# Newton steps moved to GpSimd, zero-padded queries, a sixth weight place and an earlier projection in a two-layer encoder

## The chip, the cores and the metric

The kernel runs on one core of a Trainium2 chip. The metric is the device time of one execution in microseconds; the median of the timed runs is compared. TensorE (PE in the profile) multiplies, VectorE (DVE) and ScalarE (ACT) do the elementwise work, GpSimd (POOL) clears tiles, makes small copies and issues some DMAs, and SyncE (SP) issues most DMAs.

## What is computed

Two layers are applied to 512 prompt rows and 32 sample rows of width 1024, in fp32. The sample rows also attend to 256 cached rows. Each layer has four sublayers, and each is wrapped in an RMSNorm before and after:

```python
def layer(h, p, ...):
    h = h + FFN_RES * rmsnorm(swiglu(rmsnorm(h, g_ff1_pre), w_ff1_gu, w_ff1_down), g_ff1_post)
    m, state = token_mix(rmsnorm(h, g_mix_pre), q_pos, past, w_in, ...)
    h = h + rmsnorm(m, g_mix_post)
    h = h + FFN_RES * rmsnorm(swiglu(rmsnorm(h, g_ff2_pre), w_ff2_gu, w_ff2_down), g_ff2_post)
    gate = jax.nn.sigmoid(rmsnorm(h, g_ple_pre) @ w_ple_gate)
    h = h + rmsnorm((p @ w_ple_proj) * gate, g_ple_post)
```

`token_mix` makes one input projection and runs three groups of heads on it: A, stick-breaking attention with 4 heads of width 64; B, latent attention with 8 heads, whose query comes from a projection `cq` of width 256 that is normed and projected again; and C, forgetting attention with 4 heads of width 64. The groups' outputs are normed and projected by `w_out`. The new keys, values and latents are outputs too.

## The kernel before

Activations are kept transposed: the model width lies on the partitions in 8 tiles of 128, and the 544 rows lie in the free dimension. Those columns are worked on in two parts, 0 to 256 and 256 to 544 (`HALVES`), so that one part's norm can run while TensorE multiplies the other.

Each fp32 product is three passes of a rounded type (`gemm`, lines 238 to 240): a weight and an input are each split into a high and a low part, and high by high, high by low and low by high are added in PSUM. `wh`, `wl`, `wx`, `wy` and `pb` are places for split weights and `xa`, `xb` are the input's parts. A weight is loaded into `raw` by SP, its high part is copied by ScalarE (line 109) and its low part subtracted by VectorE (line 113). A string of letters per phase (`MIX_RING` and the like) says which places follow each other; "p" is a `pb` tile. The `pb` tiles serve the attention weights later.

`Normed` and `Finish` do the norms. `Finish.fill` (lines 303, 304) adds a finished sublayer to `h` and `Normed.chunk` (258, 259) splits the next input, block by block. Sums of squares come from line 211. The factor of a norm (one over the root of the mean square) is made by `rstd` in most places: TensorE sums over partitions into a few columns (165, 167), VectorE makes an integer first guess in three operations (171 to 173) and then three Newton rounds of three operations (175 to 177) on a tile of 128x2 or 96x3, and TensorE turns the result into a row and spreads it (179). There are 20 such calls. Another form, `rstd_wide`, uses ScalarE's logarithm (186 to 200). SwiGLU's products with the factor follow in 346, 348 and 349.

In the mixer, `QK` makes queries and keys of A and C: one projection holds two heads of 64, and the result is scaled on eviction (531, 533) into one tile `kf` of the `m` pool, head 0 in rows 0 to 63, head 1 in rows 64 to 127. `attend_pair` then multiplies query and key for two heads and blocks of 128 queries (395), adds a mask by another matmul (402), and goes on to the softmax. For B, the same line reads 128 rows. In A and C the second head's matmul is held in program order.

The mixer's start takes jobs one by one, with the first part of the columns ahead of the second: queries and keys of A, values of A, and the latent's first projection `cq_job(0, ...)`; the latent's second, `cq_job(1, ...)`, comes later. A scheduler orders the instructions of each engine by its own time simulation, and an engine runs its instructions in that order. `rstd` asks for priority (300).

Of the kernel before, what the change touches and what calls it, by code (L numbers as in the profile page):

```python
# [35 lines left out]
def trunk(ctx: ExitStack, tc, a, outs, depth=2):  # L36
# [6 lines left out]
    MIX = (dict(col=16, st=1, kf=2, lq=2, s=2, cs=1, cb=1, kl=1, bq=1, rk=1), dict(m=14), dict(t=5), dict(pb=4), dict(pa=2))  # L43
# [36 lines left out]
    FFN_RING, DOWN_RING, MIX_RING = "xxyyhhhxx", "hhhxxxx", "hhpph"  # L80
# [73 lines left out]

    def rstd(out, acc, n, last=None, rc=None):
# [5 lines left out]
        with tc.high_priority(300):  # L161
# [12 lines left out]
            for _ in range(3):  # L174
                tt(e, rc, rc, op=ALU.mult)
                tt(e, e, v, op=ALU.mult)
                stt(rc, e, 1.5, rc, op0=ALU.add, op1=ALU.mult)
# [202 lines left out]
    def attend_pair(cb, kind, heads, o, chunk, vget, extra=None):  # L380
# [4 lines left out]
        for b in range(2):  # L385
# [4 lines left out]
            for i in (2 * b, 2 * b + 1):  # L390
# [3 lines left out]
                for e, (_, (q, k)) in enumerate(heads):  # L394
                    one = mm(ss[e][:, 0:w], q[:, q0:q0 + 128], k[:, 0:w], start=True, stop=False)  # L395
                    if e and kind != "B":
                        hold(one)
# [81 lines left out]
    def mix(l, h, x, g_next):  # L479
# [37 lines left out]
        class QK:  # L517
            def __init__(s, col0, scale, slot, dst=None):
                s.col0, s.scale, s.slot, s.dst, s.w = col0, scale, slot, dst, None

            def half(s, i, pbank=prj):
                c0, c1 = HALVES[i]
                if s.w is None:
                    s.w = proj(s.col0)
                    s.kf = unit("m")
                n = c1 - c0
                p = pbank()[:, 0:n]
                gemm(p, s.w, x.xh, x.xl, (c0, c1))
                t = s.kf[:, c0:c1]
                if s.scale == 1.0:  # L530
                    tt(t, p, x.r(c0, c1), op=ALU.mult)
                else:
                    stt(t, p, s.scale, x.r(c0, c1), op0=ALU.mult, op1=ALU.mult)
                if c1 == T:
                    copy(sn[:, s.slot, :], s.kf[:, SEQ:T])
                    if s.dst is not None:
                        nc.gpsimd.dma_start(out=s.dst, in_=s.kf)
# [33 lines left out]
        def attend_qk(kind, js, c, chunk, v, extra=None):  # L571
            q, k = js[c]
            heads = []
            for e in range(2):
                r = slice(e * 64, e * 64 + 64)
                heads.append((2 * c + e, tuple(z.kf[r, 0:SEQ] for z in (q, k))))
# [53 lines left out]
        cq_job(0, 0, fbank)  # L630
        rows_rstd(2, 5)
# [4 lines left out]
        cq_job(0, 1, fbank)  # L636
        set_ring("hhh")
# [235 lines left out]
        set_ring("hhhpp")  # L873
# [233 lines left out]
```

## Time and profile before

| what | value |
|---|---|
| timed runs | 2454.08, 2455.56, 2456.77 us (median 2455.56) |
| profiled execution | 2452.86 us, span 2451.1 us |
| TensorE busy, granted clock | 2382.6 us (97%), 0.985 of full speed |
| VectorE, ScalarE, GpSimd busy | 1379.4 (56%), 1025.6 (42%), 48.8 us (2%) |

Busy time is the time in which the engine had an instruction in work. A low share for GpSimd says that there is room on it, not what its instructions cost. TensorE's share is an average, so what it waits for has to be read stage by stage. The timed runs lie within 2.7 us of each other.

### The profile page before, as it was taken

To read this page: it belongs to the slowest core of one execution; us is meant where nothing else is said; L and a number is where in the kernel's file an instruction comes from. 1 tells how busy PE (TensorE), PEld (TensorE's weight loads), DVE (VectorE), ACT (ScalarE), POOL (GpSimd) and SP (SyncE) were. 2 spreads that over 40 slices of the span, in tenths; PEclk is the share of its full clock that TensorE was granted. 3 is DMA by queue.
4 is the path that set the end of the run, shared out by engine and by line. 5 is a ranking of instruction groups with operands and counts; after the bars stand their busy time and mean duration, and the time that the engine had idled before them with its cause. 6 is when DMAs were issued, how large, how long until landed. Compare 5 with 4: busy or idle time off the path is not lost.

```text
span 2451.1 us, 43918 instructions
## 1 busy us (share of the span) xinstructions
PE 2382.6 (97%) x18022; PEld 2253.3 (92%) x18022; DVE 1379.4 (56%) x3052; ACT 1025.6 (42%) x2163; POOL 48.8 (2%) x116
## 2 busy tenths in 40 slices
PE   8999999999998999999999999999999989999997
PEld 8999999886688999999999999998865989999997
DVE  6344446765757344446863444476667663444466
ACT  5322224566754322224533222245677543222243
POOL 0000000110000000000000000001100000000000
PEclk9999999999998999999999999999999999999998
DMA  5322322222023322322213223122211233323221
GB/s 160 111 81 86 105 70 72 93 88 59 23 80 107 104 88 83 101 85 87 84 47 96 95 80 102 54 94 86 89 51 44 81 94 105 95 75 104 81 70 37
DMA packets 72376, 204.99 MB, mean 84 GB/s; under 512 B 9248, under 2 KB 18088, under 8 KB 72176
## 3 DMA queue, kind: packets, MB, share of 16 engines
q1 hardware_dynamic: 69072, 193.57, 25.4%
q0 software_dynamic: 3104, 8.62, 1.1%
q8 instruction: 141, 2.31, 0.4%
q14 instruction: 59, 0.48, 0.1%
HBM read 188.21 MB, written 11.85 MB: 82 GB/s over the span
## 4 chain that ended last, share of the span: by engine, by line
PE 92%; DVE 4%; DMA 2%; ACT 1%; issue 0%; SPq 0%; DVEq 0%; ACTq 0%
PE acc L238 12%; PE acc L239 12%; PE acc L240 12%; PE prj L238 10%; PE prj L239 10%; PE prj L240 10%; PE pv L238 4%; PE pv L239 4%; PE pv L240 4%; PE acc L395 3%; PE pv L414 2%; PE tr L135 2%; DMA raw<-in_w_ff_gu_dram 1%; DVE z L303 1%; PE prj L556 1%; PE prj L557 1%
## 5 line engine op out<-in xcount | busy, mean ns | idle before, releaser
L109 ACT ACTIVATE wh<-raw 128x1024 fp32r<-128x1024 f32 (+3 forms) x157 | 151.1, 965 | 247.5 <-PE acc L239 108.1
L109 ACT ACTIVATE wx<-raw 128x1024 fp32r<-128x1024 f32 (+3 forms) x149 | 139.5, 936 | 266.4 <-PE acc L239 100.2
L113 DVE TENSOR_TENSOR wl<-raw,wh 128x1024 fp32r<-128x1024 f32 (+3 forms) x157 | 173.6, 1107 | 80.0 <-ACT wh L109 79.3
L113 DVE TENSOR_TENSOR wx<-raw,wx 128x1024 fp32r<-128x1024 f32 (+3 forms) x149 | 159.4, 1070 | 75.1 <-ACT wx L109 74.9
L238 PE MATMUL prj<-xa,wh 128*128 128x256 f32 (+3 forms) x632 | 187.8, 297 | 4.6 <-DVE q L346 2.7
L239 PE MATMUL prj<-xb,wh 128*128 128x256 f32 (+3 forms) x632 | 187.1, 296 | 4.1 <-DVE xb L259 4.1
L109 ACT ACTIVATE m<-q 128x256 fp32r<-128x256 f32 (+1 forms) x192 | 81.9, 431 | 255.0 <-DVE q L349 252.7
L240 PE MATMUL prj<-xa,wl 128*128 128x256 f32 (+3 forms) x632 | 184.3, 292 | 0.0
L238 PE MATMUL acc<-xa,wx 128*128 128x256 f32 (+1 forms) x600 | 174.4, 291 | 5.7 <-ACT wx L109 5.7
L239 PE MATMUL acc<-xb,wx 128*128 128x256 f32 (+1 forms) x600 | 173.8, 290 | 0.0
L240 PE MATMUL acc<-xa,wx 128*128 128x256 f32 (+1 forms) x600 | 173.4, 289 | 0.0
L239 PE MATMUL acc<-xb,wh 128*128 128x288 f32 (+1 forms) x576 | 167.4, 291 | 0.0
L240 PE MATMUL acc<-xa,wl 128*128 128x288 f32 (+1 forms) x576 | 166.8, 290 | 0.0
L238 PE MATMUL acc<-xa,wh 128*128 128x288 f32 (+1 forms) x576 | 166.6, 292 | 0.0
L240 PE MATMUL prj<-xa,wx 128*128 128x288 f32 (+1 forms) x480 | 139.5, 291 | 1.3 <-DVE wx L113 1.3
L238 PE MATMUL prj<-xa,wx 128*128 128x288 f32 (+1 forms) x480 | 140.6, 293 | 0.0
L239 PE MATMUL prj<-xb,wx 128*128 128x288 f32 (+1 forms) x480 | 140.3, 292 | 0.0
L347 ACT ACTIVATE q<-q 128x256 f32<-128x256 f32 (+1 forms) x176 | 74.1, 425 | 143.3 <-DVE q L346 140.8
L239 PEld LDWEIGHTS prj<-xb,wh 128*128 128x128 f32 (+1 forms) x632 | 120.1, 190 | 7.7 <-DVE xb L259 5.9
L238 PEld LDWEIGHTS prj<-xa,wh 128*128 128x128 f32 (+1 forms) x632 | 120.1, 190 | 7.7 <-DVE q L346 3.2
L240 PE MATMUL acc<-xa,wy 128*128 128x288 f32 (+1 forms) x424 | 122.7, 289 | 0.7 <-DVE wy L113 0.7
L238 PE MATMUL acc<-xa,wy 128*128 128x288 f32 (+1 forms) x424 | 123.3, 291 | 0.0
(500 smaller groups left out, 7802.5 us busy)
## 6 DMA issues: line engine op xcount, KB each, us to landing
raw<-in_w_ff_gu_dram SPq DMA_DIRECT2D x174, 512.0 KB, 3.5
raw<-in_w_ff_down_dram SPq DMA_DIRECT2D x64, 384.0 KB, 3.1
raw<-in_w_ff_down_dram SPq DMA_DIRECT2D x64, 320.0 KB, 2.9
raw<-in_w_in_dram SPq DMA_DIRECT2D x22, 512.0 KB, 3.5
raw<-in_w_out_dram SPq DMA_DIRECT2D x16, 512.0 KB, 3.4
raw<-in_w_ple_gate_dram SPq DMA_DIRECT2D x16, 512.0 KB, 3.4
raw<-in_w_v_dram SPq DMA_DIRECT2D x8, 512.0 KB, 3.4
t<-dh SPq DMA_DIRECT2D x16, 144.0 KB, 3.0
```

What stands on the lines that cost most here:

```text
L109: act(out, in_, AF.Copy)
L113: tt(lo, src, f(hi), op=ALU.subtract)
L135: nc.tensor.transpose(out, in_, ident[0:n, 0:n])
L238: mm(p, wh[k], xh[k][:, c0:c1], start=i == 0, stop=False)
L239: mm(p, wh[k], xl[k][:, c0:c1], start=False, stop=False)
L240: mm(p, wl[k], xh[k][:, c0:c1], start=False, stop=i == len(ks) - 1)
L303: stt(t, s.y[c][:, c0:c1], s.g[c], s.R[c0], op0=ALU.mult, op1=ALU.mult)
L347: act(g, g, AF.Silu)
L395: one = mm(ss[e][:, 0:w], q[:, q0:q0 + 128], k[:, 0:w], start=True, stop=False)
L414: one = mm(O[64 * e:64 * e + 64, qs], vget(hd, j), pts[e][:, j, qs], start=j == 0, stop=j == end, skip_group_check=True)
L556: mm(p, x.xh[k][:, c0:c0 + n], s.wh[k], start=k == 0, stop=False)
L557: mm(p, x.xl[k][:, c0:c0 + n], s.wh[k], start=False, stop=False)
```

## The change

Four things are changed. In `rstd`, each Newton round's three VectorE operations become four on GpSimd: the last, which added a constant and multiplied by a tensor, is made of two. The first guess stays on VectorE. A query of group A or C gets two tiles of full height instead of one shared by two heads: each holds one head in its own rows and zeros, set by GpSimd, in the others. The key tile stays shared, so that zeros meet the other head's key. The eviction of such a query is two operations of 64 rows. The hold on the second head's matmul goes. The `m` pool has 11 tiles instead of 14, `kf` one instead of two. The mixer's weight string gets a sixth place, "p", and `pb` six tiles instead of four. `cq_job(1, ...)` moves into the mixer's start.

```diff
--- before.py
+++ after.py
@@ -40,7 +40,7 @@
     COMMON = dict(xa=8, xb=8, y=8, h=8, raw=2, wh=3, wl=3, q=6, z=3, sq=2, r=5, n=6, rc=2)
     COMMON_PS = dict(tr=2, acc=3, prj=2, pv=1)
     FFN = (dict(wx=8), dict(m=12, ph=4), dict(wy=4))
-    MIX = (dict(col=16, st=1, kf=2, lq=2, s=2, cs=1, cb=1, kl=1, bq=1, rk=1), dict(m=14), dict(t=5), dict(pb=4), dict(pa=2))
+    MIX = (dict(col=16, st=1, kf=1, lq=2, s=2, cs=1, cb=1, kl=1, bq=1, rk=1), dict(m=11), dict(t=5), dict(pb=6), dict(pa=2))
     where, count, alias = {}, [0], {}
 
     def open_pools(st, sb_tags, ps_tags, tag):
@@ -77,7 +77,7 @@
             s.st.close()
 
     ring, wn, bn = [], [0], [0]
-    FFN_RING, DOWN_RING, MIX_RING = "xxyyhhhxx", "hhhxxxx", "hhpph"
+    FFN_RING, DOWN_RING, MIX_RING = "xxyyhhhxx", "hhhxxxx", "hhpphp"
     RING_TAGS = dict(x=("wx", "wx"), y=("wy", "wy"), h=("wh", "wl"), p=("pb", "pb"))
 
     def set_ring(names):
@@ -151,6 +151,8 @@
             off += n
         bfs.append(at.pop("b_f")[0])
         gains.append(at)
+
+    ptt, pts = nc.gpsimd.tensor_tensor, nc.gpsimd.tensor_scalar
 
     def rstd(out, acc, n, last=None, rc=None):
 
@@ -172,9 +174,10 @@
             ts(rc.bitcast(I32), v.bitcast(I32), 1, MASK, op0=ALU.arith_shift_right, op1=ALU.bitwise_and)
             ts(rc.bitcast(I32), rc.bitcast(I32), -1, MAGIC, op0=ALU.mult, op1=ALU.add)
             for _ in range(3):
-                tt(e, rc, rc, op=ALU.mult)
-                tt(e, e, v, op=ALU.mult)
-                stt(rc, e, 1.5, rc, op0=ALU.add, op1=ALU.mult)
+                ptt(e, rc, rc, op=ALU.mult)
+                ptt(e, e, v, op=ALU.mult)
+                pts(e, e, 1.5, None, op0=ALU.add)
+                ptt(rc, rc, e, op=ALU.mult)
             for i in range(k):
                 mm(t[:, i * m:i * m + m], rc[:, i:i + 1].to_broadcast([m, 128]), ident[0:m, 0:m], start=True, stop=True)
             if out is None:
@@ -392,9 +395,7 @@
                 w = max(nk, 256) if extra else nk
                 ss = [bank("acc") for _ in heads]
                 for e, (_, (q, k)) in enumerate(heads):
-                    one = mm(ss[e][:, 0:w], q[:, q0:q0 + 128], k[:, 0:w], start=True, stop=False)
-                    if e and kind != "B":
-                        hold(one)
+                    mm(ss[e][:, 0:w], q[:, q0:q0 + 128], k[:, 0:w], start=True, stop=False)
                 for e, s in enumerate(ss):
                     if extra:
                         lq, rk = lqs[e]
@@ -517,24 +518,29 @@
         class QK:
             def __init__(s, col0, scale, slot, dst=None):
                 s.col0, s.scale, s.slot, s.dst, s.w = col0, scale, slot, dst, None
+                s.rows = [slice(0, 64), slice(64, 128)] if dst is None else [slice(0, 128)]
 
             def half(s, i, pbank=prj):
                 c0, c1 = HALVES[i]
                 if s.w is None:
                     s.w = proj(s.col0)
-                    s.kf = unit("m")
+                    s.kf = [unit("m") for _ in s.rows]
+                    if len(s.rows) == 2:
+                        for e in range(2):
+                            nc.gpsimd.memset(s.kf[e][s.rows[1 - e], 0:SEQ], 0.0)
                 n = c1 - c0
                 p = pbank()[:, 0:n]
                 gemm(p, s.w, x.xh, x.xl, (c0, c1))
-                t = s.kf[:, c0:c1]
-                if s.scale == 1.0:
-                    tt(t, p, x.r(c0, c1), op=ALU.mult)
-                else:
-                    stt(t, p, s.scale, x.r(c0, c1), op0=ALU.mult, op1=ALU.mult)
-                if c1 == T:
-                    copy(sn[:, s.slot, :], s.kf[:, SEQ:T])
-                    if s.dst is not None:
-                        nc.gpsimd.dma_start(out=s.dst, in_=s.kf)
+                R = x.r(c0, c1)
+                for t, r in zip(s.kf, s.rows):
+                    if s.scale == 1.0:
+                        tt(t[r, c0:c1], p[r, :], R[r, :], op=ALU.mult)
+                    else:
+                        stt(t[r, c0:c1], p[r, :], s.scale, R[r, :], op0=ALU.mult, op1=ALU.mult)
+                    if c1 == T:
+                        copy(sn[r, s.slot, :], t[r, SEQ:T])
+                if c1 == T and s.dst is not None:
+                    nc.gpsimd.dma_start(out=s.dst, in_=s.kf[0])
 
         def qk_jobs(qcol, kcol, scale, slot, dst):
             return [(QK(qcol + 128 * c, scale, slot + c),
@@ -572,8 +578,7 @@
             q, k = js[c]
             heads = []
             for e in range(2):
-                r = slice(e * 64, e * 64 + 64)
-                heads.append((2 * c + e, tuple(z.kf[r, 0:SEQ] for z in (q, k))))
+                heads.append((2 * c + e, (q.kf[e][:, 0:SEQ], k.kf[0][:, 0:SEQ])))
             attend_pair(cb, kind, heads, o, chunk, v.get, extra)
 
         def cache_kv(kname, vname):
@@ -628,12 +633,14 @@
         for t in range(2):
             va.tile(t, fbank)
         cq_job(0, 0, fbank)
+        cq_job(1, 0, fbank)
         rows_rstd(2, 5)
         ja[0][0].half(1, fbank)
         ja[0][1].half(1, fbank)
         for t in range(2, 5):
             va.tile(t, fbank)
         cq_job(0, 1, fbank)
+        cq_job(1, 1, fbank)
         set_ring("hhh")
         cs, cb, kl = mix_constants()
         attend_qk("A", ja, 0, 0, va)
@@ -870,7 +877,7 @@
         gb = group_norm((2, 3, 4, 5), 512, "h")
         on = {**ga, **gc, **gb}
 
-        set_ring("hhhpp")
+        set_ring("hhhppp")
         acc = unit("r")
         y = [None] * KD
         order = [0, 1, 6, 7, 2, 3, 4, 5]
```

Line numbers move by 2 or 3 and more after the change: the first guess is at 173 to 175, the Newton steps at 177 to 180, the broadcast at 182, the fill at 306, 307, 262, 214, SwiGLU's products at 349, 351, 352, and the head matmuls at 398.

Here is the order on VectorE at the start of the second FFN in the first layer, before the change, from the first Newton step on. `rc` and `n` are the small tiles of the call, `wl` the low part of a weight, `z`, `y` and `xb` the tiles of the fill.

```order
L175 TENSOR_TENSOR n_8632<-rc_8379 128x2
L113 TENSOR_TENSOR wl_8735<-raw_8732,wh_8734 128x1024
L303 SCALAR_TENSOR_TENSOR z_8468<-y_7840,gt_77,r_7833 128x288
L303 SCALAR_TENSOR_TENSOR z_8476<-y_7874,gt_77,r_7833 128x288
L176 TENSOR_TENSOR n_8632<-n_8632,n_8631 128x2
L304 TENSOR_TENSOR y_7840<-t_8470,z_8468 128x288
L304 TENSOR_TENSOR y_7874<-t_8478,z_8476 128x288
L177 SCALAR_TENSOR_TENSOR rc_8379<-n_8632,rc_8379 128x2
L113 TENSOR_TENSOR wl_8801<-raw_8798,wh_8800 128x1024
```

The Newton steps stand one by one among weight splits and the fill. After the change, the same place from the first guess's last operation (175) on:

```order
L175 TENSOR_SCALAR rc_8409<-rc_8409 128x2
L203 SCALAR_TENSOR_TENSOR r_7863<-z_8494,z_8491 128x288
L113 TENSOR_TENSOR wl_8768<-raw_8765,wh_8767 128x1024
L306 SCALAR_TENSOR_TENSOR z_8498<-y_7870,gt_77,r_7863 128x288
L306 SCALAR_TENSOR_TENSOR z_8506<-y_7904,gt_77,r_7863 128x288
L307 TENSOR_TENSOR y_7870<-t_8500,z_8498 128x288
L307 TENSOR_TENSOR y_7904<-t_8508,z_8506 128x288
L113 TENSOR_TENSOR wl_8834<-raw_8831,wh_8833 128x1024
```

The nine steps are gone from VectorE, and the rest follows in the same sequence. The result is made by GpSimd, where the first round of this call stands behind two DMA issues:

```order
L791 DMA h_6870<-in_cache_b_ckv_dram 128x256
L736 DMA q_6495<-in_cache_c_logf_dram 4x256
L177 TENSOR_TENSOR n_8662<-rc_8409 128x2
L178 TENSOR_TENSOR n_8662<-n_8662,n_8661 128x2
L179 TENSOR_SCALAR n_8662<-n_8662 128x2
L180 TENSOR_TENSOR rc_8409<-rc_8409,n_8662 128x2
```

Two more such rounds follow it, with nothing between the twelve steps, and each waits for the one before it.

The second place is the first SwiGLU products that need the factor (`q` from 346 and 348), on VectorE too. Before, they stand here, after most of the fill's second part:

```order
L303 SCALAR_TENSOR_TENSOR z_8516<-y_8103,gt_77,r_7833 128x288
L259 SCALAR_TENSOR_TENSOR xb_8373<-y_8067,gt_77,xa_8365 128x288
L304 TENSOR_TENSOR y_8103<-t_8518,z_8516 128x288
L211 TENSOR_TENSOR r_8377<-r_8377,z_8513 128x288
L303 SCALAR_TENSOR_TENSOR z_8526<-y_8139,gt_77,r_7833 128x288
L346 TENSOR_TENSOR q_8624<-prj_8574,r_8378 128x256
L348 TENSOR_TENSOR q_8625<-pv_8575,r_8378 128x256
L346 TENSOR_TENSOR q_8718<-acc_8668,r_8378 128x256
L348 TENSOR_TENSOR q_8719<-prj_8669,r_8378 128x256
```

After the change, the same products (349, 351) stand here:

```order
L262 SCALAR_TENSOR_TENSOR xb_8400<-y_7904,gt_77,xa_8392 128x288
L214 TENSOR_TENSOR r_8407<-r_8407,z_8513 128x288
L307 TENSOR_TENSOR y_7996<-t_8518,z_8516 128x288
L113 TENSOR_TENSOR wx_8840<-raw_8837,wx_8839 128x1024
L349 TENSOR_TENSOR q_8654<-acc_8604,r_8408 128x256
L351 TENSOR_TENSOR q_8655<-prj_8605,r_8408 128x256
L349 TENSOR_TENSOR q_8751<-acc_8701,r_8408 128x256
L306 SCALAR_TENSOR_TENSOR z_8526<-y_8061,gt_77,r_7863 128x288
L351 TENSOR_TENSOR q_8752<-acc_8702,r_8408 128x256
```

They have moved ahead of the fill, from behind tile 6 of 8 of the fill (`y_8103`) to behind tile 3 of 8 (`y_7996`) and a weight split.

The third place is TensorE at the mixer's start in the first layer, where the first part of the columns ends and the second (128x288) begins. `prj_4969` is A's first query projection, `acc_4924` the latent's first. Before:

```order
L238 MATMUL acc_4924<-xa_4570,wh_4917 128x256
L239 MATMUL acc_4924<-xb_4578,wh_4917 128x256
L240 MATMUL acc_4924<-xa_4570,wl_4918 128x256
L238 MATMUL prj_4969<-xa_4563,wh_4760 128x288
L239 MATMUL prj_4969<-xb_4571,wh_4760 128x288
L240 MATMUL prj_4969<-xa_4563,wl_4761 128x288
```

After the change, `acc_4934` is the latent's first projection, `prj_4972` its second, with its weights in `pb`, and `prj_5087` the values of the next rows:

```order
L242 MATMUL acc_4934<-xb_4584,wh_4927 128x256
L243 MATMUL acc_4934<-xa_4576,wl_4928 128x256
L241 MATMUL prj_4972<-xa_4576,pb_4966 128x256
L242 MATMUL prj_4972<-xb_4584,pb_4966 128x256
L243 MATMUL prj_4972<-xa_4576,pb_4967 128x256
L562 MATMUL prj_5087<-pb_4859,xa_4569 128x256
L563 MATMUL prj_5087<-pb_4859,xb_4577 128x256
```

The latent's second projection now runs in the first part, beside the first, and the value projection of the second part starts ahead of A's query.

## Rows read from the trace of the kernel before

**Rows 1.** The page: busy time by engine, and the chain that ended last, by engine.

```profile
PE 2382.6 (97%) x18022; PEld 2253.3 (92%) x18022; DVE 1379.4 (56%) x3052; ACT 1025.6 (42%) x2163; POOL 48.8 (2%) x116
...
PE 92%; DVE 4%; DMA 2%; ACT 1%; issue 0%; SPq 0%; DVEq 0%; ACTq 0%
```

**Rows 2.** Waits of TensorE: line waited for: us in total, times, longest us.

```profile
PE tr L179 <- DVE rc L177: 18.2, 3, 8.3
...
PE prj L239 <- DVE xb L259: 4.1, 7, 1.0
PE tr L179 <- DVE n L177: 3.0, 2, 2.4
PE prj L238 <- DVE q L346: 2.7, 2, 1.3
...
PE prj L238 <- ACT xa L258: 1.9, 2, 1.1
```

**Rows 3.** Timeline of TensorE, first mixer: start us, us, engine, line, operation, shapes.

```profile
471.02 0.30 PE L238 MATMUL prj<-xa,wh 128*128 128x288 f32 x1
471.25 1.12 PE L395 MATMUL acc<-m,m 64*128 64x512 f32 x2
472.31 0.23 PE L402 MATMUL acc<-cb 128*128 128x128 bf16 x1
...
514.42 0.49 PE L395 MATMUL acc<-m,m 64*128 64x128 f32 x4
...
608.33 0.28 PE L240 MATMUL prj<-m,wl 128*128 128x256 f32 x1
608.45 1.02 PE L395 MATMUL acc<-xb,m 128*128 128x512 f32 x2
609.31 0.22 PE L402 MATMUL acc<-cb 128*128 128x128 bf16 x1
```

**Rows 4.** Line 395, head matmuls: duration ns min/median/max, first and last start, forms.

```profile
L395 PE MATMUL acc<-m,m x128: 272/481/694, 456.4 to 1805.2; 64*128 64x256 f32 x48, 64*128 64x384 f32 x32, 64*128 64x512 f32 x32, 64*128 64x128 f32 x16
```

**Rows 5.** Busy us of PE, PEld, DVE, ACT, POOL; granted clock, DMA share, GB/s.

```profile
490.00:540.00 50.00, 50.00 (x361) 42.70 (x360) 35.15 (x72) 30.38 (x71) 11.14 (x28) 1.00 0.29 93
750.00:760.00 10.00, 1.22 (x4) 0.93 (x4) 9.53 (x25) 5.35 (x11) 0.00 (x0) 0.62 0.55 171
760.00:770.00 10.00, 9.59 (x62) 9.59 (x63) 8.75 (x24) 5.54 (x13) 0.00 (x0) 0.70 0.01 2
```

**Rows 6.** Timeline of VectorE, second FFN's start, first layer.

```profile
743.54 0.15 DVE L171 TENSOR_SCALAR n<-tr 128x2 f32<-128x2 f32 x1
...
744.96 0.15 DVE L175 TENSOR_TENSOR n<-rc 128x2 f32<-128x2 f32 x1
...
759.94 0.42 DVE L346 TENSOR_TENSOR q<-prj,r 128x256 f32<-128x256 f32 x1
```

**Rows 7.** Groups on GpSimd: busy us, mean ns of one, idle before.

```profile
L645 POOL MEMSET rk<- 128x512 f32 x2 | 1.1, 553 | 0.0
```

**Rows 8.** Timeline of TensorE, second FFN's start, both layers; idle time in brackets.

```profile
757.86 1.22 PE L179 MATMUL tr<-cst,rc 128*128 128x128 f32 x4 [8.30 <-DVE rc L177]
760.41 0.58 PE L238 MATMUL prj<-xa,wh 128*128 128x256 f32 x1 [1.33 <-DVE q L346]
...
1974.78 1.23 PE L179 MATMUL tr<-cst,rc 128*128 128x128 f32 x4 [6.89 <-DVE rc L177]
```

**Rows 9.** Line 669, copies on GpSimd: duration ns min/median/max.

```profile
L669 POOL COPY s<-kl x32: 202/204/507, 489.5 to 1712.6; 32x32 f32<-32x32 f32 x32
```

**Rows 10.** Line 669 in three stretches: length, GpSimd busy (records), clock, DMA, GB/s.

```profile
490.00:491.45 1.45, 1.29 (x3) 1.00 0.82 308
491.45:492.20 0.75, 0.61 (x3) 1.00 0.09 27
```

**Rows 11.** Timeline at the end, VectorE and TensorE.

```profile
2438.25 0.16 DVE L175 TENSOR_TENSOR n<-n 96x3 f32<-96x3 f32 x1
...
2440.00 1.59 PE L179 MATMUL tr<-cst,n 96*128 96x96 f32 x6 [2.38 <-DVE n L177]
```

## The prediction

> **What bounds the kernel now.** I read the page first, for who is busy and which chain ended last. TensorE is busy 97% of the span and makes up 92% of the chain; GpSimd is busy for 48.8 us of 2451 [rows 1]. So time can come from two places only: matmuls that take longer than their columns need, and the 68 us or so (2451.1 less 2382.6) in which TensorE does nothing. Next I read what TensorE waited for, longest first [rows 2]: the broadcast of the Newton result is at the top, 18.2 us in 3 waits and 3.0 in 2 more, then the second half of the normed input at the mixer's start (4.1 us on xb, 1.9 on xa), and two waits of 2.7 in all for the first SwiGLU tiles. A few waits hold much of it, so I opened each in the timeline. Last I compared head matmuls of the 64-wide groups, which read 64 rows, with those of the latent group, which read 128 [rows 3]. A change in 64 matmuls can't be seen in shares; it must be counted.
>
> The sum is made against the profiled execution, 2452.86 us (span 2451.1 and 1.76 around it). The median of the timed runs is 2455.56, 2.7 higher; what is saved is taken off that. Anything within 0.2%, 4.9 us, counts as no change.
>
> **Zero rows under the 64-wide queries.** The lone 64-row matmul of 512 columns starts 0.23 after its predecessor's start (471.02 to 471.25) and the next matmul starts 1.06 later. The full-height one starts 0.12 after its predecessor and is followed after 0.86 (608.45 to 609.31) [rows 3]. Each predecessor alone is worth 0.13 and 0.12 (288 and 256 columns at the steps in the same rows' neighbours), so the difference is 0.10 + 0.20 = 0.30 us, although a full-height one multiplies twice the rows. The record count says 128, two passes each, so 64 matmuls [rows 4]; one row of adjacent heads is shown, four records in 0.43 us at 514.42 [rows 3], and I found four such pairs in the order. The other 56 stand alone: 56 x 0.295 = 16.5 us. The adjacent ones win nothing: four full-height passes of 128 columns at 0.11 would take 0.44. TensorE has no idle time here (50.00 of 50 us [rows 5]), so a shorter matmul moves the rest forward; but heads also wait for softmax pieces, and some of those waits will appear. I take 14.5; bounds 0 (the extra time belongs to something else than the row count) and 16.5.
> What it adds: 16 more evictions on VectorE of some 0.42 us (the row at 759.94 of 256 columns [rows 6]), 6.7 us in stretches where VectorE is busy 35 of 50 us [rows 5]; hidden by the 15 idle ones. Without that cover they would cost 6.7. Sixteen memsets at about 0.55 [rows 7] run on GpSimd, which is idle; the eight small ScalarE copies likewise go into idle time.
>
> **Newton steps on GpSimd.** VectorE runs nine steps per call, one at a time between other work. At the second FFN's start of the first layer they begin at 744.96, the sums having been read at 743.54 [rows 6], and the broadcast is released only at 757.86 after 8.30 us of idle TensorE; a further 1.33 follows until the first SwiGLU product. In the second layer the same stall is 6.89 [rows 8]. Between those two times VectorE does 9 x 0.16 = 1.4 us of Newton and 11.5 of something else: in the order shown, 21 other instructions are queued between the steps. On GpSimd nothing else is queued.
> The price p of one dependent GpSimd step isn't in the trace. From below: the 32x32 copies, 204 ns in the median [rows 9], start at every 0.25 us in a stretch in which VectorE is idle (three in 0.75). From above: three copies filled 1.29 of a 1.45 us stretch in which VectorE ran two-input operations, 0.43 each [rows 10], the longest 507 ns. VectorE itself was not slower there. I take p = 0.40, nearer the upper row, since VectorE is crowded wherever the result is urgent. Twelve steps: 4.8 us.
> At the two FFN starts: the seed is ready at about 744.7, plus 0.3 to hand over and 4.8, so 749.8 instead of 757.8: 8.0 earlier. In the changed order the SwiGLU products also stand directly behind a weight split, before the rest of the fill, so the 1.33 doesn't grow. The slow clock behind the stall (granted 0.62 and 0.70 of full speed in the two stretches after 750 [rows 5]) cost 2 to 3 us more. Against that, the fill of the second half ends no sooner, at about 766, so TensorE meets that next. I take 8.5 and, from 6.89, 6.5: 15 for both layers. Bounds 8 (p = 0.60 and the fill late) and 22 (8.30 + 1.33 + 6.89 + 1.33 and some 4 of clock).
> The other calls: of 20, three more waited before, 3.05, 0.62 and 2.38 us (the rest of the two sums in [rows 2]). From the changed order I counted the matmuls between a call's last sum and its broadcast, at 0.118 and 0.130 each: 17 calls (without the two above and the last) have 4.6 to 7.7 us, 109.5 in all. A call needs 2.2 + 12p: 0.5 for the sums, 0.6 to 1.4 for three VectorE steps (743.54 to 744.96 [rows 6]), up to 1.2 behind a weight split. At p = 0.40 that is 7.0, which exceeds 11 of the windows, by 11.1 us together; less the 3.05 and 0.62 gone, +7. At p = 0.30 it is 1.6 - 3.7 = -2; at 0.50, 29.9 - 3.7 = +26. In these places the Newton work has so far been hidden by TensorE's queue, and it is the length of that queue which decides.
> The last call has no cover. VectorE was idle and took nine steps from 2438.25 to 2440.00 [rows 11], 1.75; twelve at 0.27 take 3.2, and the handover 0.1: +1.6. Bounds 0.5 and 4.
> The rule against this edit is in the Trainium skill, "GPSIMD Engine Reference", section 4.1 Engine selection: elementwise work belongs on VectorE, since GpSimd is about twice as slow on two-input operations. No run here shows such an operation. An estimate by that factor of two, from VectorE's 0.156 us, is p = 0.31, and the sum would then be about 2420.
>
> **The second latent query projection and the sixth place.** At the mixer's start TensorE waits some 6.0 us over both layers for xb and xa [rows 2]. The change puts 24 matmuls of 256 columns, 2.8 us each layer, in front of the second half, with one more weight place so that the load is there in time. But its split and evictions add about 2.5 us of VectorE work ahead of the last xb, and VectorE is what TensorE waits for. On SP one weight load goes ahead of the eight stores of h; those are read later. I take 3; bounds 0 and 6 (all of the wait), and a loss of the same 2.5 each layer, 5, if VectorE has no gap. The fewer m places cost nothing by the order, which issues the group's work as before.
>
> **Sum.** -14.5 - 15 + 7 + 1.6 - 3 = -23.9: 2429 for a profiled execution like the one shown, 2431 or 2432 for the median.
>
> **The rivals.**
> *GpSimd steps are dear.* The 17 windows are the place: each loses 12 times what p exceeds. At p = 0.50 the sum is -14.5 - 12.6 + 26.2 + 2 - 3 = -1.9, no change; at 0.60 it is -14.5 - 10 + 46.6 + 3 - 3 = +22, 2478. It decides from 0.51. For it speaks the 507 ns copy; against it the median over 32 copies [rows 9]. Chance 0.17, of which 0.12 slower and 0.05 no change.
> *Padding is worth nothing*, because the time between the heads is a wait that moves along, or the extra row comes from the weights. Then -9.4, 2446. Against it speaks that the full-height matmuls differ in rows alone. Chance 0.13, of which 0.03 no change. Beside it the Trainium skill, "TensorEngine Tiling (Array Packing)", Key Properties, says that row halves can multiply in parallel, which padding gives up. By that, the four adjacent pairs would lose up to 0.22 each, some 0.9 us; the row at 514.42 shows four passes in 0.43, no gain from it.
> *Everything pays.* p near 0.25, the queues cover all calls: 16.5 + 18 + 4 of clock + 3.7 + 3 less 1.5, about -44, 2412. Chance 0.13.
> *The forecast*, p between 0.3 and 0.48 and padding paying: -35 to -12, 2420 to 2444. Chance 0.57.
>
> **How the numbers follow.** The likeliest gives 2431. Below 2412 I leave 1 in 10, for clock and fill that gain more together; above 2453, the price where the rival starts, 1 in 10. Faster by over 0.2% (under 2450.7): 0.57 + 0.13 + 0.10 = 0.80. Within 0.2%: 0.05 + 0.03 = 0.08. Slower: 0.12.
>
> **What would show it.** Head matmuls of 512 columns with 64-wide heads followed after 0.86 and not 1.06, led in by 0.13; nothing left of the 8.30 and 6.89 at the two FFN starts but 1 to 2 us, and a granted clock near 1.00 in the 10 us after them; GpSimd rows of 0.2 to 0.4 us, and 3.5 to 5 us from seed to broadcast; new waits of the broadcast, each under 2.5 us, in some ten other calls, adding up to 5 to 12; about 4 us of idle TensorE before the last broadcast; and 3 to 5 us of waits left at the mixer's start. I am wrong if the steps take over 0.5 us each, or if the padded heads' time reappears as waits for softmax pieces.

## The result, and the profile after

The changed kernel takes 2413.86 us in the median (2410.14 to 2415.59 in 4 runs), the kernel before 2454.82 beside it: a ratio of 0.9833, with a 95% interval of 0.9821 to 0.9846. It is 41 us faster. That is inside the range, at its lower end, 17 us under the likeliest time and close to the rival in which everything pays. The profiled execution took 2415.59 us, with a span of 2413.7; it is the slowest of the four, so the traces show 37.4 of the 41 us.

The page after the change (busy time by engine, the chain that ended last, by engine), beside [rows 1]:

```profile
PE 2352.9 (97%) x18022; PEld 2245.7 (93%) x18022; DVE 1366.0 (57%) x2888; ACT 1025.1 (42%) x2171; POOL 140.1 (6%) x372
...
PE 91%; DVE 3%; DMA 2%; POOL 1%; ACT 1%; issue 1%; SPq 0%; DVEq 0%; POOLq 0%; ACTq 0%
```

TensorE has as many instructions and is busy 29.7 us less. So most of the gain is time in which a matmul was in work, at a mean granted clock of 0.991 instead of 0.985, and only 7.7 us are idle time. The waits of TensorE, beside [rows 2]:

```profile
PE tr L182 <- POOL rc L180: 8.2, 5, 4.2
...
PE acc L562 <- ACT h L567: 5.3, 1, 5.3
PE prj L562 <- ACT y L567: 5.3, 1, 5.3
...
PE tr L182 <- POOL n L180: 4.7, 1, 4.7
```

The broadcast still waits 12.9 us, where it waited 21.2, but in other places: 4.23 and 2.84 at the second FFNs, 4.67 at the end, and only 1.2 in three more calls (0.38, 0.25 and 0.55). At each mixer's start there is one wait of 5.3, where there were 3.1 and 2.9 us before, in pieces of at most 1.1. The three longest waits of the broadcast on TensorE's timeline (idle time in brackets), beside [rows 8, 11]:

```profile
744.68 1.22 PE L182 MATMUL tr<-cst,rc 128*128 128x128 f32 x4 [4.23 <-POOL rc L180]
...
1937.16 0.71 PE L182 MATMUL tr<-cst,rc 128*128 128x128 f32 x4 [2.84 <-POOL rc L180]
...
2402.57 1.60 PE L182 MATMUL tr<-cst,n 96*128 96x96 f32 x6 [4.67 <-POOL n L180]
```

In the ten microseconds around the first of them the granted clock is 0.67, and 0.99 in the next ten (busy us of PE, PEld, DVE, ACT and POOL, then the clock), where it was 0.62 and 0.70 in [rows 5]. These are means of the two levels that the traces show, 0.5 and 1.0 of full speed (1.2 and 2.4 GHz):

```profile
740.00:750.00 10.00, 5.77 (x29) 5.57 (x29) 8.03 (x17) 6.76 (x14) 4.22 (x6) 0.67 0.61 191
750.00:760.00 10.00, 10.00 (x81) 10.00 (x81) 8.64 (x22) 4.28 (x11) 0.00 (x0) 0.99 0.12 35
```

Since the same matmuls run in the same number in every kernel, stretches can be compared by the start of a given high-by-high matmul (line 238 before, 241 after), counted in order of time: number 1000 stands in the first FFN, 1380 in the second FFN's first part of layer 0, 2000 in its middle, 3600 in layer 1's first FFN, 4000 and 4900 likewise in layer 1's second. Its times in us, and the span, read from the traces of the kernels named (their edits are below):

```
                        1000   1380   2000    3600    4000    4900    span
before                 392.6  717.8  970.5  1601.1  1934.4  2291.0  2451.1
changed                394.1  710.1  956.3  1577.7  1901.9  2252.2  2413.7
newton_alone           394.7  718.5  964.4  1591.8  1924.3  2275.1  2436.6
newton_back_on_vector  392.2  710.3  962.7  1593.3  1916.9  2272.8  2433.4
padding_alone          393.8  709.5  961.9  1595.1  1919.0  2275.7  2435.9
queries_unpadded       394.3  718.7  964.8  1590.6  1921.6  2270.3  2432.1
unpadded_free_order    393.8  717.4  960.5  1585.0  1916.2  2263.7  2425.2
changed_beside         393.9  710.3  954.0  1575.0  1899.2  2249.5  2411.4
projection_back        394.3  713.3  958.3  1585.2  1907.1  2255.3  2417.1
five_places            393.9  712.0  957.0  1583.9  1907.7  2258.0  2419.7
ends_on_vector         393.1  709.6  956.3  1577.3  1901.9  2252.2  2412.5
ends_beside            392.4  708.3  954.8  1576.8  1900.5  2250.9  2410.9
fine_splits            393.5  709.6  955.0  1581.5  1905.0  2255.0  2415.4
```

Each column less the one before it is a stretch; compared with before, the changed kernel gains 9.3 and 9.1 us in the two mixers (1000 to 1380, 3600 to 4000), 6.5 and 6.3 at the two second FFNs' starts (1380 to 2000, 4000 to 4900), 9.1 from there to layer 1 (2000 to 3600), and loses 1.5 ahead of all that and 1.4 at the end. Between such places the difference stands still.

`changed_beside` is the changed kernel traced a second time. Six of its seven stretches are within 0.5 us of the first trace's, but at the start of layer 0's second FFN the gain is 8.9 us instead of 6.5. There the broadcast waits less, because the chain on GpSimd took 6.0 us instead of 7.9, and the granted clock from 740 to 750 is 0.83 instead of 0.67:

```profile
743.31 0.71 PE L182 MATMUL tr<-cst,rc 128*128 128x128 f32 x4 [2.67 <-POOL rc L180]
```

The two traces of the kernel with three calls on VectorE (`ends_on_vector`, `ends_beside`) differ by up to 1.0 us in a stretch and by 1.4 in the two mixers together. The kernel before was traced once. Differences of this size between two kernels are not told from chance here.

### The profile page after: what moved, and what is told of

Read it like the earlier page. It is cut to its first block, busy times and chain, and to the rows that moved or that the text cites. A ratio compares the mean times of both kernels' runs of the same rounds, so it can differ in the third digit from the quotient of the medians.

```text
span 2413.7 us, 44086 instructions
## 1 busy us (share of the span) xinstructions
PE 2352.9 (97%) x18022; PEld 2245.7 (93%) x18022; DVE 1366.0 (57%) x2888; ACT 1025.1 (42%) x2171; POOL 140.1 (6%) x372
## 4 chain that ended last, share of the span: by engine, by line
PE 91%; DVE 3%; DMA 2%; POOL 1%; ACT 1%; issue 1%; SPq 0%; DVEq 0%; POOLq 0%; ACTq 0%
PE acc L241 12%; PE acc L242 12%; PE acc L243 12%; PE prj L241 10%; PE prj L242 10%; PE prj L243 10%; PE pv L241 4%; PE pv L242 4%; PE pv L243 4%; PE acc L398 3%; PE pv L415 2%; PE tr L135 2%; DMA raw<-in_w_ff_gu_dram 1%; PE prj L562 1%; DMA raw<-in_w_ple_gate_dram 1%
## 5 line engine op out<-in xcount | busy, mean ns | idle before, releaser
L113 DVE TENSOR_TENSOR wl<-raw,wh 128x1024 fp32r<-128x1024 f32 (+4 forms) x153 | 168.7, 1104 | 81.6 <-ACT wh L109 80.5
L241 PE MATMUL acc<-xa,wx 128*128 128x288 f32 (+1 forms) x664 | 193.9, 293 | 5.7 <-ACT wx L109 5.7
L243 PE MATMUL acc<-xa,wx 128*128 128x288 f32 (+1 forms) x664 | 193.5, 292 | 0.7 <-DVE wx L113 0.7
L242 PE MATMUL acc<-xb,wx 128*128 128x288 f32 (+1 forms) x664 | 193.6, 292 | 0.0
L242 PE MATMUL acc<-xb,wh 128*128 128x256 f32 (+1 forms) x600 | 173.4, 289 | 0.7 <-DVE xb L262 0.7
L241 PE MATMUL acc<-xa,wh 128*128 128x256 f32 (+1 forms) x600 | 172.2, 290 | 0.4 <-ACT xa L261 0.2
L243 PE MATMUL acc<-xa,wl 128*128 128x256 f32 (+1 forms) x600 | 172.3, 288 | 0.0
L241 PE MATMUL prj<-xa,wh 128*128 128x288 f32 (+3 forms) x560 | 166.0, 297 | 0.0
L242 PE MATMUL prj<-xb,wh 128*128 128x288 f32 (+3 forms) x560 | 164.8, 294 | 0.0
L241 PE MATMUL prj<-xa,wx 128*128 128x256 f32 (+1 forms) x480 | 138.8, 289 | 0.0
L243 PE MATMUL prj<-xa,wx 128*128 128x256 f32 (+1 forms) x480 | 138.0, 288 | 0.0
L241 PEld LDWEIGHTS acc<-xa,wx 128*128 128x128 f32 x664 | 125.4, 189 | 6.7 <-ACT wx L109 6.4
L243 PEld LDWEIGHTS acc<-xa,wx 128*128 128x128 f32 x664 | 126.1, 190 | 1.4 <-DVE wx L113 1.1
```

Source lines behind the costliest of these rows:

```text
L113: tt(lo, src, f(hi), op=ALU.subtract)
L241: mm(p, wh[k], xh[k][:, c0:c1], start=i == 0, stop=False)
L242: mm(p, wh[k], xl[k][:, c0:c1], start=False, stop=False)
L243: mm(p, wl[k], xh[k][:, c0:c1], start=False, stop=i == len(ks) - 1)
```

## Experiments

Times are medians, beside the kernel before on the same chip.

**The Newton steps: undone, and alone.**

```diff
-                ptt(e, rc, rc, op=ALU.mult)
-                ptt(e, e, v, op=ALU.mult)
-                pts(e, e, 1.5, None, op0=ALU.add)
-                ptt(rc, rc, e, op=ALU.mult)
+                tt(e, rc, rc, op=ALU.mult)
+                tt(e, e, v, op=ALU.mult)
+                stt(rc, e, 1.5, rc, op0=ALU.add, op1=ALU.mult)
```

`newton_back_on_vector` makes this edit in the changed kernel, `newton_alone` its reverse in the kernel before.

> The changed kernel with the Newton steps back on VectorE, the rest kept. Theory A (the plateaus of the two traces: the steps are worth 12.7 us at the two second FFNs, 9.1 around the per-layer embedding of the first layer, and cost 1.5 at the start and 1.4 at the end): about 19 us slower than the changed kernel, some 2433. Theory B (the forecast's terms: 15 gained, 8.6 lost): about 6 us slower, 2420, and the rest of the gain stays.

> The kernel before with the Newton steps on GpSimd and nothing else. Theory A: 19 us faster than before, about 2436, with the mixers as long as before. Theory B: 6 us faster, 2448.

Measured: 2435.3 (0.9931, 0.9916 to 0.9946) and 2436.6 (0.9934, 0.9920 to 0.9949), before 2453.29. With the steps undone, 18 of the 41 us remain; doing it alone gains 17. Theory A holds, the forecast's terms (B) fall. In the table, `newton_alone` gains 6.7 and 5.8 at the second FFNs and 3.1 from there to layer 1, where the changed kernel gains 9.1 and `newton_back_on_vector` nothing. So all of the 9.1 needs the steps on GpSimd, but 6 of it needs something else too.

**The padded queries: undone, undone without the hold, and alone.** In the changed kernel, for `queries_unpadded`:

```diff
-                s.rows = [slice(0, 64), slice(64, 128)] if dst is None else [slice(0, 128)]
+                s.rows = [slice(0, 128)]
...
-                heads.append((2 * c + e, (q.kf[e][:, 0:SEQ], k.kf[0][:, 0:SEQ])))
+                r = slice(e * 64, e * 64 + 64)
+                heads.append((2 * c + e, tuple(z.kf[0][r, 0:SEQ] for z in (q, k))))
...
-                    mm(ss[e][:, 0:w], q[:, q0:q0 + 128], k[:, 0:w], start=True, stop=False)
+                    one = mm(ss[e][:, 0:w], q[:, q0:q0 + 128], k[:, 0:w], start=True, stop=False)
+                    if e and kind != "B":
+                        hold(one)
```

`unpadded_free_order` leaves the last piece out. `padding_alone` makes the change's edits to `QK` and `attend_pair` in the kernel before, with its pools.

> The changed kernel with one query tile for two heads again (64-row head matmuls, second head held in order), the rest kept, the smaller pool too. Theory A (56 lone head matmuls at 0.295 us): 16 us slower than the changed kernel, about 2430. Rival (the mixers gained 18.6 us from the weight place and the earlier projection): within 4 us of the changed kernel.

> The changed kernel with 64-row head matmuls and one query tile for two heads, but without the hold on the second head. Theory A (the row count is the cost): the mixers take as long as with the hold, 7 to 8 us each more than in the changed kernel. Rival (the freed order is what the mixers gain by): within 2 us of the changed kernel's mixers.

> The kernel before with the padded query tiles and no hold, nothing else (pools of before). Theory A (each lone 64-row matmul costs 0.295 us more): 15 to 16.5 us faster than before, about 2438, all of it in the two mixers, between the first FFN's end and the second FFN's start. Rival (part of the mixers' gain comes from the weight place and the projection): 8 us or less.

Measured: 2434.61 (0.9921, 0.9906 to 0.9936), 2432.51 (0.9919, 0.9905 to 0.9932; before 2451.21 there) and 2436.55 (0.9936, 0.9922 to 0.9949; before 2452.61). Without padding, with the hold or free of it, the mixers are within 2.3 us of before; with padding alone they gain 9.6 and 9.4. So the rows are the cost, not the order of heads, and the rival that gives the mixers' gain to the weight place and the projection falls. The totals are not the mixers alone. `queries_unpadded` came out slower than expected, since it also lost 4.4 us between 2000 and 3600, and `padding_alone` gains 16.1 and not 19, since it lost 2.7 there. In the 120 us where that happens its waits of TensorE add up to 8.4 us, as before (8.6), but the granted clock is 0.93 instead of 0.96. The trace of `unpadded_free_order` is of its fastest execution, 2426.94. A lone padded matmul of the changed kernel, on TensorE's timeline, beside [rows 3]:

```profile
473.93 0.28 PE L242 MATMUL prj<-xb,wh 128*128 128x256 f32 x1
474.05 1.02 PE L398 MATMUL acc<-m,m 128*128 128x512 f32 x2
474.91 0.22 PE L403 MATMUL acc<-cb 128*128 128x128 bf16 x1
```

It starts 0.12 after its predecessor and is followed after 0.86, exactly as a matmul of the latent group.

**The projection and the weight place.** In the changed kernel, `projection_back` makes the first edit, `five_places` the others:

```diff
-        cq_job(1, 0, fbank)
...
-        cq_job(1, 1, fbank)
```

```diff
-    FFN_RING, DOWN_RING, MIX_RING = "xxyyhhhxx", "hhhxxxx", "hhpphp"
+    FFN_RING, DOWN_RING, MIX_RING = "xxyyhhhxx", "hhhxxxx", "hhpph"
...
-        set_ring("hhhppp")
+        set_ring("hhhpp")
```

together with four `pb` tiles instead of six.

> The changed kernel with the latent's second query projection back at its old place; the sixth weight place stays. Theory A (moved forward, it fills the sixth PSUM bank, and TensorE waits 5.3 us for the first eviction in each layer where it waited 3.1 and 2.8 before): 4 us faster than the changed kernel, about 2410. Rival (the wait is only gathered in one place, and the 24 matmuls do fill idle time): 3 to 5 us slower, about 2418.

> The changed kernel with five weight places and four tiles for them again. Its order of instructions around the per-layer embedding of the first layer is that of the kernel with the projection put back, not that of the changed kernel, although no code of that stretch differs. Theory A (some 5 us of the changed kernel's gain there is that order): 5 us slower than the changed kernel, lost there, with a wait of the broadcast of 2.7 us and a lower clock after it; the mixers as long as in the changed kernel. Rival (the gain there belongs to the Newton steps): as fast there, and the mixers 3 us or more longer for want of the place.

Measured: 2418.61 (0.9863, 0.9847 to 0.9880) and 2421.05 (0.9873, 0.9859 to 0.9886); before 2453.29 and 2452.61. Both are slower than the changed kernel, but the table shows that 5.5 us of it lies, both times, between 2000 and 3600, where neither edit changes a line. In the two mixers together the projection is worth 0.7 us (18.4 gained against 17.7) and the place 1.7, about what two traces of one kernel differ by. The sum hides that the layers differ: with the projection put back, the first mixer takes 3.0 us more and the second 2.3 less; why the signs differ is not shown. So the rival's total for `projection_back` came out, not its reason, and theory A's 4 us did not: the wait is real (TensorE, changed kernel),

```profile
440.06 0.58 PE L562 MATMUL prj<-pb,xa 128*128 128x256 f32 x1 [5.29 <-ACT y L567]
```

since TensorE has filled its banks with first-part products, none of which is evicted before the factor is there (written at 439.45 on VectorE; the first eviction starts at 439.54). With five places the wait for a bank is longer, 7.18 us in each layer. In `projection_back` it waits 3.4 us instead, in six pieces, with matmuls in between at a granted clock of 0.84 where the changed kernel has 0.98 (stretches of 10 us: busy us of PE, PEld, DVE, ACT, POOL, then the clock): it is busy for 6.57 us instead of 4.77, but with 33 matmuls instead of 39. First the changed kernel, then `projection_back`:

```profile
430.00:440.00 10.00, 4.77 (x39) 4.51 (x38) 9.48 (x28) 4.70 (x15) 0.00 (x0) 0.98 0.29 112
440.00:450.00 10.00, 9.94 (x68) 9.94 (x69) 9.35 (x24) 5.29 (x14) 2.11 (x4) 0.85 0.38 139
```

```profile
430.00:440.00 10.00, 6.57 (x33) 4.97 (x32) 9.73 (x30) 4.95 (x14) 0.97 (x2) 0.84 0.29 112
440.00:450.00 10.00, 10.00 (x69) 10.00 (x69) 7.14 (x18) 4.19 (x10) 1.15 (x3) 0.82 0.37 139
```

So the longer wait cost no matmul here; that it and the clock cancel over the whole mixer is not shown. For theory A of `five_places`, its timeline of TensorE in the stretch that differs has

```profile
1227.37 1.17 PE L182 MATMUL tr<-cst,rc 128*128 128x128 f32 x4 [2.70 <-POOL rc L180]
...
1229.47 0.58 PE L241 MATMUL acc<-xa,wy 128*128 128x256 f32 x1 [0.93 <-DVE q L349]
```

where the changed kernel has no wait of the broadcast. In the ten microseconds around it the clock of `five_places` is 0.66, and 1.00 in the changed kernel (in this order):

```profile
1225.00:1235.00 10.00, 6.70 (x32) 6.40 (x33) 6.16 (x17) 4.65 (x13) 1.82 (x7) 0.66 0.00 0
```

```profile
1217.00:1227.00 10.00, 9.54 (x78) 9.14 (x78) 8.33 (x24) 4.65 (x12) 3.78 (x14) 1.00 0.01 2
```

The two orders differ in what stands first when the per-layer embedding's last norm and the next FFN's first norm meet. In the changed kernel the next norm's sums run ahead of the other's broadcast; in `five_places` they run behind it, and the chain on GpSimd starts at 1221.46 instead of 1218.01 (TensorE, changed kernel and `five_places`):

```profile
1216.66 0.36 PE L167 MATMUL tr<-cst,r 128*128 128x2 f32 x2
1216.89 0.36 PE L169 MATMUL tr<-cst,z 128*128 128x2 f32 x2
...
1217.58 0.91 PE L182 MATMUL tr<-cst,n 96*128 96x96 f32 x6
```

```profile
1218.22 0.80 PE L182 MATMUL tr<-cst,n 96*128 96x96 f32 x6
1218.86 0.31 PE L167 MATMUL tr<-cst,r 128*128 128x2 f32 x2
```

Theory A of `five_places` holds. Every kernel here with GpSimd steps and the sums ahead gained 8.6 to 9.6 us in this stretch, without a wait of that broadcast (the changed one and the one with three calls on VectorE, each traced twice). Every one with the sums behind gained 3.1 to 6.1 and waited 1.7 to 2.7 us: `newton_alone`, `projection_back`, `five_places`, `fine_splits`, `queries_unpadded` and `unpadded_free_order`. Their orders differ in detail. The last two have the same order on TensorE and VectorE from 2000 to 3600 and gained 4.7 and 6.1, at mean granted clocks of 0.997 and 1.000, so 1.4 us of such a figure is not the order. The scheduler chose between the orders after edits far away.

**What a GpSimd step costs.** `chain_probe` adds this behind the changed kernel's last output, once for each kind of work `bg` beside it (`rc` starts at 1, `v` at -0.5):

```python
hold(ts(rc, rc, 1.0, None, op0=ALU.mult))
for _ in range(3):
    ptt(e, rc, rc, op=ALU.mult)
    ptt(e, e, v, op=ALU.mult)
    pts(e, e, 1.5, None, op0=ALU.add)
    ptt(rc, rc, e, op=ALU.mult)
for _ in range(24 if k == 2 else 12):
    bg()
```

> The changed kernel with work added after its last output: five chains of twelve GpSimd steps, alone, beside VectorE subtractions of two 128x1024 inputs, beside additions of two 128x288 inputs, beside one-input 128x1024 operations, and beside ScalarE copies. Theory A (a step next to a two-input VectorE operation ends just after it): 0.27 us a step alone and beside the one-input and ScalarE work, about 1.1 beside the subtractions, 0.4 beside the additions. Rival (the steps at the second FFN's start were slow for the DMA traffic there): 0.27 in all five.

The stretches of the chains of twelve: length, busy us of PE, PEld, DVE, ACT, POOL with records, beside 128x1024 subtractions, 128x288 additions, one-input 128x1024 operations, and alone:

```profile
2414.60:2429.62 15.02, 0.00 (x0) 0.00 (x0) 14.56 (x12) 7.68 (x8) 14.05 (x12) 0.50 0.00 1
2429.85:2435.63 5.78, 0.00 (x0) 0.00 (x0) 5.36 (x13) 0.00 (x0) 4.85 (x12) 0.50 0.00 0
2441.62:2450.23 8.61, 0.00 (x0) 0.00 (x0) 8.17 (x12) 0.00 (x0) 7.67 (x12) 0.50 0.00 0
2450.48:2453.80 3.32, 0.00 (x0) 0.00 (x0) 0.00 (x0) 0.00 (x0) 2.39 (x12) 0.50 0.00 0
```

That is 1.25, 0.48, 0.72 and 0.28 us a step. Theory A holds but for the one-input operations, which were to leave it alone and hold a step as well. The ScalarE copies did not run beside their own chain but beside the first one, whose steps kept 0.27 to 0.30. The Trainium skill, "SBUF — State Buffer", section Who interferes with whom, offers a reason: VectorE's second pair of ports is also GpSimd's and is locked by one of them at a time; a VectorE operation with two inputs in SBUF contends with GpSimd's reads through it, one in a two-port mode takes the pair for the whole instruction, and ScalarE never waits. The rows agree for the two-input operations and ScalarE; whether the one-input operations ran in such a mode, no run shows.

**The steps beside smaller operations.** `ends_on_vector`, and timed again beside the changed kernel as `ends_beside`, puts the first two and the last of the 20 calls back on VectorE:

```diff
+    calls, ON_VECTOR = [0], (1, 2, 20)
...
+        calls[0] += 1
...
+                if calls[0] in ON_VECTOR:
+                    tt(e, rc, rc, op=ALU.mult)
+                    tt(e, e, v, op=ALU.mult)
+                    stt(rc, e, 1.5, rc, op0=ALU.add, op1=ALU.mult)
+                    continue
```

> The changed kernel with three of the 20 calls' Newton steps on VectorE again: the first two and the last. Theory A (GpSimd's chain loses 1.5 us at the start and 1.4 at the end where nothing covers it): 2.9 us faster than the changed kernel, about 2411, no idle 4.67 us but 2.4 before the last broadcast. Rival (the loss at the start has another cause): 1.4 us faster.

> The kernel with the first two and the last call's Newton steps on VectorE, beside the changed kernel on one chip. Theory A (the chain on GpSimd loses where no matmul covers it): 2 us faster than the changed kernel, nearly all at the end. Rival (what it wins at the ends is lost in between): within 1 us.

> The changed kernel itself, timed beside the next two. Theory A and its rivals alike: 2411 to 2416, 1.6 to 1.8% faster than before.

Measured: 2411.1 (0.9830, 0.9816 to 0.9843; before 2452.61); side by side 2412.55 (0.9839, 0.9826 to 0.9852) and, for the changed kernel, 2413.74 (0.9847, 0.9834 to 0.9861; before 2451.21). Faster by 1 us, less than the intervals tell apart, so neither theory is decided by the total. At the end the traces agree: the wait before the last broadcast is 2.7 and 3.1 us on VectorE, 4.7 and 4.3 on GpSimd, and the stretch behind 4900 is 1.2 and 2.0 us shorter. Whether GpSimd costs anything at the start stays open. Against before, number 1000 came 1.1 to 2.1 us later in the seven traces with the first two calls on GpSimd, and in the five with these calls on VectorE from 0.4 earlier to 1.2 later (`padding_alone`).

`fine_splits` adds to it four subtractions in place of one for six weights of the second FFN:

```diff
+        if fine:
+            copy(hi, raw)
+            for i in range(0, k, 2):
+                tt(lo[:, i:i + 2, :], raw[:, i:i + 2, :], f(hi[:, i:i + 2, :]), op=ALU.subtract)
+            return hi, lo
```

> The kernel with three calls on VectorE, and with the low parts of the six weights at the start of the second FFN subtracted in four pieces of 128x256 instead of one of 128x1024. Theory A (a GpSimd step waits for the VectorE operation beside it): the chain there falls from 7.9 us to some 5, TensorE's wait from 4.2 and 2.8 us to 1 to 2, and each second FFN's start gains 2 us. Its order around the per-layer embedding of the first layer is the longer one, so 5 us are lost there. Rival (the steps wait for VectorE's queue however it is cut): the chain stays over 7 us.

Measured: 2415.91 (0.9855, 0.9841 to 0.9868). In the changed kernel, GpSimd's last steps at the second FFN are

```profile
740.40 1.07 POOL L177 TENSOR_TENSOR n<-rc 128x2 f32<-128x2 f32 x1
...
742.43 2.19 POOL L180 TENSOR_TENSOR rc<-rc,n 128x2 f32<-128x2 f32 x1
```

the first beside a weight split (740.19 to 741.42 on VectorE), the last through four VectorE operations without a gap, of which the last is a split too. The chain takes 7.9 us. In `fine_splits` no step takes over 0.45, it takes 4.3, and the broadcast waits 1.23 instead of 4.23; then the first SwiGLU product is late (the changed kernel has no wait there):

```profile
741.27 0.71 PE L189 MATMUL tr<-cst,rc 128*128 128x128 f32 x4 [1.23 <-POOL rc L187]
745.93 0.39 PE L253 MATMUL acc<-xa,wh 128*128 128x256 f32 x1 [2.88 <-DVE q L363]
```

On VectorE that product stands behind the subtraction of a weight that ended at 745.5. In the second layer the chain takes 4.2 us, the broadcast has no wait, and a SwiGLU product waits 2.46. In the other nine traces with GpSimd steps there, the chains take 5.0 to 8.2 us. So theory A holds for the chain, and its rival falls. The 2 us for each start are not seen: the stretches gain 7.3 and 6.6 us, against 6.2 and 6.2 in `ends_beside`, but the changed kernel traced twice gained 6.5 and 8.9 in the first of them. The wait moved on. The longer order between 2000 and 3600 then costs 4.5.

## Why the prediction was right, and where it was not

**Padding, -14.5.** Right in mechanism, and a little small. Alone it gains 19.0 us in the mixers; the same stretches with and without it in the changed kernel differ by 15.3. The 56 x 0.295 is 8.3 us a mixer. In the first one the 64 head records of A and C take 8.2 us less from start to start in `padding_alone` and 8.7 in the changed kernel (23.3 before), and the matmuls right before and behind them, together, 0.4 and 0.2 less. The rest of the 9.6 and 9.3 is not placed. The 2 us taken off for softmax waits didn't come.

**The second FFNs, -15.** Measured 12.8, 15.3 in the second trace of the same kernel, and 12.5 with the Newton steps alone. The size is about right, the working is not. The seed and the handover came as said, but p was no 0.40 there: 7.9 us for twelve, 0.66 each, beside splits of 128x1024. That is over the 0.5 that the prediction gave as its own sign of being wrong, and 4.23 and 2.84 us of the stall stayed, not 1 to 2. The nearest row, a copy of 507 ns, had no such operation beside it. What made up for it is what the prediction kept: both waits of 1.33 for the first SwiGLU products are gone, and TensorE never met the late fill that was to follow. The idle time of TensorE falls by 5.4 us at each of the two starts (8.30 + 1.33 to 4.23, 6.89 + 1.33 to 2.84); how much of the other 2 us the clock gave is not shown.

**The other calls, +7.** This term had the wrong sign. The price was right: 17 chains took 4.7 us in the mean, 0.39 a step, where 0.40 was taken. The windows were not. From the last sum's start to the broadcast TensorE had 126.9 us of work in those 17 calls, read from the trace, against 109.5 counted: the sums themselves, transposes and the last matmul's drain were left out, about 1 us a call. And a call needed 6.6 us, not 7.0. So the stalls left are 1.3 us in four calls, not 11.1, and the 3.7 removed are a gain. With `newton_alone` the stretch gains 3.1, but not by these 3.7: there the broadcast waits of 2.71 and 0.55 us stay. The further 5.5 to 6 go with an order, as `five_places` shows, which no term foresaw: the order of the changed kernel was there to be read, and its effect on where a chain starts was not worked out. The whole stretch before and after (length, busy us of PE, PEld, DVE, ACT, POOL, the clock):

```profile
970.50:1601.10 630.60, 622.03 (x4923) 620.63 (x4922) 328.49 (x697) 214.43 (x386) 0.00 (x0) 0.99 0.27 83
956.30:1577.70 621.40, 617.87 (x4923) 615.92 (x4922) 320.94 (x625) 213.50 (x386) 29.88 (x96) 1.00 0.28 84
```

TensorE's idle time falls by 5.0 us and its busy time by 4.2, with the same matmuls at a higher clock. So nearly as much busy time went as idle time; the term had no price for that.

**The last call, +1.6.** Measured: 4.67 of idle time instead of 2.38, and 1.4 and 1.9 by the table. Twelve steps took 3.27, against 3.2.

**Projection and place, -3.** Not shown to be anything: 0.7 and 1.7 in the mixers, inside the bounds, but hardly more than the 1.4 by which two traces of one kernel differ. The mechanism failed. The 24 matmuls were to fill idle time and leave 3 to 5 us of waits at the mixers' starts; the waits rose from 6.0 to 10.6 us, since all banks were full. That the mixers came out near the two terms together is in part luck: padding paid more, this little or nothing.

By stretches the changed kernel's traces add up to -18.4 (mixers: padding, projection, place), -12.8 (second FFNs), -9.1 (the other calls and their order), +1.4 and, at the start, +1.5: -37.4, against a sum of -23.9. The mixers and the second FFNs came within 2.2 us of their terms; the other calls, 14.6 off with the start, are the miss. The second trace adds up to -39.6, the 2.3 more nearly all at the second FFNs. So the range held, while the step from windows to stalls failed. The time is where the rival *everything pays* put it, 2412, and for half of its reason: the queues did cover nearly all calls, but p was 0.39 in these 17 calls and not near 0.25, and the second FFNs did not give its 22.

## What to carry to other kernels

When a short dependent chain is spread out in a crowded queue, an idle engine can run it sooner although each step takes longer; what it costs is read from what runs beside it, and compared with the work that the waiting engine has left, counted from start to start in the trace and not from a sum of matmuls. A matmul of 64 rows among full ones is worth timing from its predecessor's start to its successor's. Where a scheduler orders the instructions, compare an edit by stretches: part of a gain may come from an order chosen far from it, and go with the next edit.

## What was not expected of the hardware

A GpSimd step of 0.19 us took 2.19 where VectorE ran four operations without a gap beside it, so it may lose its turn more than once. This differs between executions of one kernel: in `changed_beside` the same step took 0.32. One-input VectorE operations of 128x1024 held each step for 0.72 us. Waiting can cost more than its length: `five_places` lost 5.5 us between 2000 and 3600 for 3.1 more of waiting around the broadcast (2.70 and 0.93 against 0.5), with a granted clock of 0.66 in those ten microseconds, where the changed kernel has 1.00.
